# Norm factors by transposes, and the sample tokens' state products issued four units at a time

## The chip, the cores and the metric

The kernel runs on one core of a Trainium2 chip. The metric is the device time of one execution in microseconds (us), the median of several runs. TensorE (PE in the profile; its weight loads are PEld) multiplies matrices into PSUM; VectorE (DVE), ScalarE (ACT) and GpSimd (POOL) do the rest; SP issues nearly all DMAs.

## The reference, cut to what matters

One layer of a hybrid decoder for 1024 prompt tokens and 8 x 8 sample tokens: a SwiGLU feed-forward net, a token mixer with a pooling branch and an SSD (Mamba-2) branch, a second feed-forward net, and a last norm. All is float32.

```python
def rmsnorm(x, g):
    xf = x.astype(jnp.float32)
    y = xf * lax.rsqrt(jnp.mean(xf * xf, axis=-1, keepdims=True) + EPS)
    return (y * g.astype(jnp.float32)).astype(x.dtype)
...
def step(h, inp):
    s_c, d_c = inp
    return h * d_c[..., None, None] + s_c, h
h_last, h_prev = lax.scan(step, h0, ...)
y_off = jnp.einsum('bclgn,bcgrpn,bclgr->bclgrp', cr, h_prev, jnp.exp(a_cs))
y = (y_diag + y_off)
...
yg = yg * lax.rsqrt(jnp.mean(yg * yg, axis=-1, keepdims=True) + EPS)
```

For the sample tokens `h0` is the state of each of the 8 sequences (32 heads of 64 x 128 numbers each, 8 MB in all). It is read, enters `y_off` through the products C h0, and is written back as the new state.

## The kernel before

Channels lie on the 128 partitions and tokens along the rows of a tile. The tokens are done in two halves: half 0 is 512 prompt tokens, half 1 the other 512 and the 64 sample tokens. The stages follow one another: `ffn1`, the mixer for half 0 and then half 1, `ffn2`. Dense products split each float32 operand into a high and a low part and use three products (`products`). The weights are split on ACT (`wh`, line 292) and DVE (`wl`, line 293).

**The order of the work.** The dense products are the backbone. Everything else is written as generators ("chains"). A planner clock `pe[0]` counts what was issued to TensorE: `mm` adds the moving size over 2400, times four for plain float32 operands; `tr` adds 0.107. A chain that yields d is due again when that clock has moved on by d. `tick()`, called after each group of dense products (six in half 1), runs chains that are due, and `finish` runs one to its end without waiting. The program order found so is then scheduled by the compiler, which lets later instructions of an engine pass earlier ones that are not ready in its model and fixes one order for each engine. Tiles come from shared pools: `act` gives 42 buffers of 576 columns to nearly everything in the mixer; `psum("ps", ...)` has four banks there and `psum("pd", ...)` four more for the dense products.

**Norm factors.** `rstd` squares the tiles, sums over partitions with products by `ones` (tile `pss`), takes the power on POOL (line 361), and has a column of factors for each 128 tokens in the small tile `rsm`. To multiply a tile, the factors must lie along the row, the same on every partition: `along` (line 363) does it with one TensorE instruction for each 128 tokens, whose stationary operand is the column repeated 128 times and whose moving operand is the identity. Four go into one bank `prb`, which ACT copies to `r` (line 399). In half 1 a fifth one of 64 rows goes into a corner of `pss` (line 402 copies it). `rstd` is called twelve times: once for each half before the mixer and before `ffn2`, and four times for each half in `gating`.

**The sample tokens' state.** `ssd_group` runs a group of 8 heads: four chunks of 128 prompt tokens, and in half 1 a fifth chunk, the sample tokens, whose second part is `ssd_b` with `smp` true. It has eight units: `bh` (which four sequences) times `pr` (which two heads of the group). For a unit:

- `load` issues the DMA of the state (tile `h0`, shown as `h`; line 1242), two units ahead;
- `turn` makes four transposes on TensorE into bank `ph0T` (line 168 is the body of `tr`) and copies it on ACT to `h0T` (line 1250);
- four products of `Cf` (32 columns of C) with `h0T`, one for each sequence, go to the four 32-partition quarters of bank `pyos`, in columns of unit `pr`;
- one product makes `pnew`, what the tokens add to the state; four DVE instructions (line 1273) combine it with `h0`, and a DMA stores the new state (line 1276);
- after the fourth unit (`pr == 3`) ACT copies `pyos` to `yt` (line 1279), four transposes make `pyT`, and DVE multiplies what is wanted of it into `ea` (line 1285).

`turn` of unit i+1 is called just before `pyos` of unit i, and between units stands `yield STEP_S` (2.5). In `mix_half` this chain is started beside the next group's projections (`proj_group`; conv tiles `pc`, whose raw tile `craw` POOL and ACT fill), the output product of the group before (`pso`), and the four `z` tiles (`pz`); `finish(cs)` after `z_tiles` ends it.

Of the kernel before, what the change touches and what calls it, by code (L numbers as in the profile page):

```python
# [14 lines left out]
P = 128  # L15
# [47 lines left out]
def tile_hybrid_pool_ssd_macaron(  # L63
# [19 lines left out]
    def nm(s):  # L83
        uid[0] += 1
        return f"{s}_{uid[0]}"

    def act(shape=(P, 576), dt=F32, name="a"):
        return sp.tile(list(shape), dt, tag="act", bufs=N_ACT, name=nm(name))
# [25 lines left out]
    def psum(tag="ps", name="ps"):  # L114
        npd = stage["npd"]
        return stage["ps"].tile([P, 512], F32, tag=tag, bufs=npd if tag == "pd" else 8 - npd, name=nm(name))
# [46 lines left out]
    def mm(out, lhsT, rhs, start=True, stop=True, free=False):  # L163
        T.matmul(out, lhsT, rhs, start=start, stop=stop, skip_group_check=free)  # L164
        pe[0] += max(out.free_size(), 64) / 2400.0 * (1 if rhs.dtype == F32R else 4)

    def tr(out, in_, idn):
        T.transpose(out, in_, idn)  # L168
        pe[0] += 0.107
# [7 lines left out]
    ident = cp.tile([P, P], F32, tag="ident", name="ident")  # L177
# [184 lines left out]

    def along(out, r, i, n=P):

        mm(out, r[:n, i : i + 1].broadcast_to([n, P]), ident[:n, :n])

    def rstd(tiles, h, count, out, pace=1.0):

# [28 lines left out]
        for c in range(4):  # L397
            along(pr[:, c * P : (c + 1) * P], sm[:, 0], c)
        S.copy(r[:, :512], pr)
        if h == 1:  # L400
            along(pt[:, 64:128], sm[:, 0], 4, NS)
            S.copy(r[:, 512:], pt[:, 64:128])
# [821 lines left out]
    def ssd_b(h, g, c, a, hold, Cf, y4, dts):  # L1224

        dt, acs, dtd, cd, cdp = dts
        abs_, xp, xd, ea, btok, L, tok = a
        smp = c == 4
        hc = c * NH + g * HPG
        hcs = slice(hc, hc + HPG)  # L1230
        ysl = y4[:, :, tok]
        first = h == 0 and c == 0
        if smp:
            units = [(pr, bh) for bh in range(2) for pr in range(4)]

            def src(u):
                gp = g * 4 + u[0]
                return state_ssm[0, u[1] * 4 : u[1] * 4 + 4, 2 * gp : 2 * gp + 2].rearrange("b h p n -> (h p) b n")

            def load(u):  # L1240
                t = act((P, 4, P), name="h0")
                dma(t, src(u))
                return t

            def turn(h0):
                pt = psum("ps", "ph0T")
                for b in range(4):
                    tr(pt[:, b * P : (b + 1) * P], h0[:, b, :], ident)
                hT = act((P, 4, P), name="h0T")
                S.copy(hT.rearrange("p b n -> p (b n)"), pt)  # L1250
                return hT

            h0s = {0: load(units[0]), 1: load(units[1])}
            yield STEP_S
            hTs = {0: turn(h0s[0])}
            for i, (pr, bh) in enumerate(units):
                if i + 2 < len(units):
                    h0s[i + 2] = load(units[i + 2])
                yield STEP_S
                if i + 1 < len(units):  # L1260
                    hTs[i + 1] = turn(h0s[i + 1])
                hT, h0 = hTs.pop(i), h0s.pop(i)
                gp = g * 4 + pr


                if pr == 0:
                    po = psum("ps", "pyos")
                for b in range(4):
                    mm(po[b * 32 : (b + 1) * 32, pr * P : (pr + 1) * P], Cf[:, 512 + bh * 32 : 544 + bh * 32], hT[:, b, :])
                pn = psum("ps", "pnew")  # L1270
                mm(pn, xd[bh][0][:, pr * P : (pr + 1) * P], xd[bh][1].rearrange("p b n -> p (b n)"))
                for b in range(4):
                    V.scalar_tensor_tensor(h0[:, b, :], h0[:, b, :], cdp[0][:, gp, bh * 4 + b : bh * 4 + b + 1],
                                           pn[:, b * P : (b + 1) * P], op0=ALU.mult, op1=ALU.add)
                dst = new_ssm_s[0, bh * 4 : bh * 4 + 4, 2 * gp : 2 * gp + 2].rearrange("b h p n -> (h p) b n")
                dma(dst, h0)
                if pr == 3:
                    yt = act((P, 512), name="yt")
                    S.copy(yt, po)
                    pt = psum("ps", "pyT")  # L1280
                    for k in range(4):
                        tr(pt[:, k * P : (k + 1) * P], yt[:, k * P : (k + 1) * P], ident)
                    own = bass.AP(pt.tensor, pt.offset, [list(pt.ap[0]), [P, 4], [40, 4], [1, NT]])
                    e = ea[:, :, bh * 32 : (bh + 1) * 32].rearrange("p q (b t) -> p q b t", t=NT)
                    V.tensor_tensor(e, own, e, op=ALU.mult)
        elif not first:
            po = psum("ps", "pyo")
            for pr in range(4):
                mm(po[:, pr * L : (pr + 1) * L], hold[:, pr * P : (pr + 1) * P], Cf[:, tok])
        py = psum("ps", "pyd")  # L1290
        for i in range(HPG):
            m_ = abs_[i // abs_[0].shape[1]][:L, i % abs_[0].shape[1], :]
            hh = slice((i % 2) * HD, (i % 2 + 1) * HD)
            mm(py[hh, (i // 2) * L : (i // 2 + 1) * L], xp[:L, i * HD : (i + 1) * HD], m_)
        pyv = py[:, : 4 * L].rearrange("p (q l) -> p q l", l=L)
        if first:
            V.tensor_tensor(ysl, ysl, pyv, op=ALU.add)
        else:
            if not smp:
                V.tensor_tensor(ea, po.rearrange("p (q l) -> p q l", l=L), ea, op=ALU.mult)  # L1300
            V.tensor_tensor(ea, ea, pyv, op=ALU.add)
            V.tensor_tensor(ysl, ysl, ea, op=ALU.add)
# [22 lines left out]
    def ssd_group(h, g, Bf, Cf, xs4, y4, dts):  # L1325
# [6 lines left out]
        for c in range(4 + h):  # L1332
            ga = ssd_a(h, g, c, Bf, Cf, xs4, dts)
            next(ga)
            yield step
            try:
                next(ga)
            except StopIteration as e:
                a = e.value
            yield step  # L1340
            if prev:
                for w in ssd_b(h, g, *prev, Cf, y4, dts):
                    yield w
            prev = (c, a, ssd_st(h, g, c, a, dts))
        yield step
        for w in ssd_b(h, g, *prev, Cf, y4, dts):
            yield w
# [266 lines left out]
```

## Time and profile before

| | us |
|---|---|
| median of three runs | 2942.32 |
| lowest and highest | 2939.81, 2942.77 |
| profiled execution, device time | 2938.48 |
| its span, first to last instruction | 2936.7 |
| mean granted clock of TensorE | 0.997 |

A row of the timeline gives start, length, engine, line of the code, operation, output and inputs, the shape and the number of instructions merged into it; in square brackets the idle time of the engine ahead of it and what ended that. All engine operations of TensorE go through two helpers, `mm` (line 164) and `tr` (line 168), so rows are told apart by the tile they write. Lengths of single matmuls overlap, since their ends are modelled; what a run of them costs is the time from its first start to the start of what follows.

### The profile page before, as it was taken

Reading aid. Unit: us, or ns where it says so; the run is one execution under the profiler, and the core shown is the slowest. Engines: PE = TensorE matmul, PEld = TensorE weight load, DVE = VectorE, ACT = ScalarE, POOL = GpSimd, SP = SyncE. Lnnn points to the kernel's source line nnn. Section 1 sums busy time; section 2 is a strip of 40 time slices with the busy share of each in tenths; the row PEclk is TensorE's granted clock in tenths of the full one; section 3 lists DMA queues with packets and bytes.
Section 4 is the critical chain, followed back from the end, with each engine's and each line's share of the span. In section 5 each row is a group of like instructions: output and inputs, shape, how many; then the busy total and the mean of one; then the engine's idle time right before and its main releaser. Section 6 shows DMA issues by size and latency. Waiting matters only on the chain. (4 is left out here: it accounts for less than half of the span.)

```text
span 2936.7 us, 50272 instructions
## 1 busy us (share of the span) xinstructions
PE 2887.0 (98%) x18676; PEld 2628.6 (90%) x18676; DVE 1702.4 (58%) x3172; ACT 1206.3 (41%) x2456; POOL 531.0 (18%) x642
## 2 busy tenths in 40 slices
PE   7999999999999999999999999999999999999998
PEld 6999999789988888788999988998999999997898
DVE  6655555434273897777633776867665554453432
ACT  5444444423243665443432444443234444443422
POOL 6444444000000000000000010100035444440000
PEclk9999999999999999999999999999999999999999
DMA  4565554854335888678434556556574532236652
GB/s 133 167 224 182 165 173 133 280 188 137 103 98 174 274 257 267 194 226 289 118 97 151 172 179 187 164 162 180 168 249 154 162 103 75 84 98 211 213 165 72
DMA packets 542267, 501.25 MB, mean 171 GB/s; under 512 B 36388, under 2 KB 391780, under 8 KB 542014
## 3 DMA queue, kind: packets, MB, share of 16 engines
q1 hardware_dynamic: 542006, 498.03, 54.3%
q8 instruction: 147, 2.41, 0.3%
q14 instruction: 98, 0.80, 0.1%
q10 hardware_dynamic: 16, 0.00, 0.0%
HBM read 355.94 MB, written 142.20 MB: 170 GB/s over the span
## 5 line engine op out<-in xcount | busy, mean ns | idle before, releaser
L293 DVE TENSOR_TENSOR wl<-wraw,wh 128x512 fp32r<-128x512 f32 (+1 forms) x416 | 284.5, 685 | 423.5 <-ACT wh L292 408.2
L292 ACT ACTIVATE wh<-wraw 128x512 fp32r<-128x512 f32 (+1 forms) x416 | 256.7, 618 | 637.3 <-PE po L164 235.9
L164 PE MATMUL pw<-X,wh 128*128 128x288 f32 (+1 forms) x1416 | 354.0, 329 | 4.8 <-ACT v L574 3.8
L164 PE MATMUL pw<-X,wl 128*128 128x288 f32 (+1 forms) x936 | 268.7, 287 | 0.0
L164 PEld LDWEIGHTS pw<-X,wh 128*128 128x128 f32 x1416 | 237.6, 188 | 26.8 <-ACT v L574 4.6
L164 PE MATMUL pc<-hl,wh 128*128 128x288 f32 (+1 forms) x1152 | 257.0, 330 | 0.0
L164 PE MATMUL pw<-hl,wh 128*128 128x512 f32 x608 | 220.4, 397 | 0.0
L458 DVE TENSOR_TENSOR wl<-s,wh 128x512 fp32r<-128x512 f32 x168 | 129.9, 774 | 146.4 <-ACT wh L457 124.9
L164 PE MATMUL po<-hh,wh 128*128 128x288 f32 (+1 forms) x800 | 210.4, 323 | 3.4 <-ACT hh L353 3.2
L164 PE MATMUL po<-hh,wl 128*128 128x288 f32 (+1 forms) x800 | 210.2, 322 | 0.4 <-DMA wl<-part 0.4
L164 PE MATMUL po<-hr,wh 128*128 128x288 f32 (+1 forms) x800 | 210.4, 322 | 0.0
L164 PE MATMUL pg<-hl,wh 128*128 128x288 f32 (+1 forms) x864 | 201.6, 338 | 0.8 <-issue 0.8
L164 PEld LDWEIGHTS pc<-hl,wh 128*128 128x128 f32 x1152 | 184.0, 188 | 18.9 <-issue 4.2
L164 PE MATMUL pw<-hi,wh 128*128 128x288 f32 x640 | 189.1, 295 | 1.2 <-ACT t L610 1.2
L164 PE MATMUL pw<-hi,wl 128*128 128x288 f32 x640 | 188.4, 294 | 0.0
L164 PE MATMUL pw<-lo,wh 128*128 128x288 f32 x640 | 188.4, 294 | 0.0
L164 PEld LDWEIGHTS pw<-X,wl 128*128 128x128 f32 x936 | 176.5, 189 | 0.0
L164 PE MATMUL pz<-hl,wh 128*128 128x288 f32 (+1 forms) x768 | 172.2, 333 | 0.0
L164 PE MATMUL pw<-hl,wl 128*128 128x256 f32 x608 | 169.7, 279 | 0.0
L164 PE MATMUL pc<-hl,wl 128*128 128x288 f32 (+1 forms) x576 | 157.6, 327 | 0.0
L164 PEld LDWEIGHTS pg<-hl,wh 128*128 128x128 f32 x864 | 141.2, 189 | 15.6 <-issue 2.5
L458 DVE TENSOR_TENSOR wl<-wraw,wh 128x512 fp32r<-128x512 f32 x126 | 100.2, 795 | 88.7 <-ACT wh L457 82.4
(375 smaller groups left out, 6886.3 us busy)
## 6 DMA issues: line engine op xcount, KB each, us to landing
wh<-part SPq DMA_DIRECT2D x204, 256.0 KB
wl<-part SPq DMA_DIRECT2D x204, 256.0 KB
wraw<-in_ffn_w_in_dram SPq DMA_DIRECT2D x188, 256.0 KB
wraw<-in_w_in_dram SPq DMA_DIRECT2D x180, 256.0 KB
wraw<-in_ffn_w_out_dram SPq DMA_DIRECT2D x120, 256.0 KB
part<-wh SPq DMA_DIRECT2D x112, 256.0 KB
part<-wl SPq DMA_DIRECT2D x112, 256.0 KB
ab<-acsd SPq DMA_DIRECT2D x64, 256.0 KB
```

The source lines that it names most:

```text
L164: T.matmul(out, lhsT, rhs, start=start, stop=stop, skip_group_check=free)
L292: S.activation(wh, raw, AF.Copy)
L293: V.tensor_tensor(wl, raw, wh.bitcast(F32), op=ALU.subtract)
L458: V.tensor_tensor(wl, a, wh.bitcast(F32), op=ALU.subtract)
```

## The change

`along` calls `tr` in place of `mm`, with the same operands. In `ssd_b` the turn of a unit is called ahead of the pause before its own `pnew`, the turned states of four units are kept in a dictionary by `pr`, and when `pr == 3` bank `pyos` is taken and all sixteen products of the four units are issued in a row, unit by unit. A `yield 1.0` stands between the copy to `yt` and the transposes of it.

```diff
     def along(out, r, i, n=P):
 
-        mm(out, r[:n, i : i + 1].broadcast_to([n, P]), ident[:n, :n])
+        tr(out, r[:n, i : i + 1].broadcast_to([n, P]), ident[:n, :n])
...
             h0s = {0: load(units[0]), 1: load(units[1])}
+            hTs = {}
             yield STEP_S
-            hTs = {0: turn(h0s[0])}
             for i, (pr, bh) in enumerate(units):
                 if i + 2 < len(units):
                     h0s[i + 2] = load(units[i + 2])
+                hTs[pr], h0 = turn(h0s[i]), h0s.pop(i)
                 yield STEP_S
-                if i + 1 < len(units):
-                    hTs[i + 1] = turn(h0s[i + 1])
-                hT, h0 = hTs.pop(i), h0s.pop(i)
                 gp = g * 4 + pr
-                if pr == 0:
-                    po = psum("ps", "pyos")
-                for b in range(4):
-                    mm(po[b * 32 : (b + 1) * 32, pr * P : (pr + 1) * P], Cf[:, 512 + bh * 32 : 544 + bh * 32], hT[:, b, :])
                 pn = psum("ps", "pnew")
                 mm(pn, xd[bh][0][:, pr * P : (pr + 1) * P], xd[bh][1].rearrange("p b n -> p (b n)"))
...
                 dma(dst, h0)
                 if pr == 3:
+                    po = psum("ps", "pyos")
+                    for q in range(4):
+                        for b in range(4):
+                            mm(po[b * 32 : (b + 1) * 32, q * P : (q + 1) * P], Cf[:, 512 + bh * 32 : 544 + bh * 32], hTs[q][:, b, :])
+                    hTs = {}
                     yt = act((P, 512), name="yt")
                     S.copy(yt, po)
+                    yield 1.0
                     pt = psum("ps", "pyT")
```

## The prediction

> **What bounds the kernel now.** I read the page's busy shares first, then the busy time by stretch, then what TensorE (PE) waited for.
>
> ```profile
> span 2936.7 us, 50272 instructions
> PE 2887.0 (98%) x18676; PEld 2628.6 (90%) x18676; DVE 1702.4 (58%) x3172; ACT 1206.3 (41%) x2456; POOL 531.0 (18%) x642
> ...
> PE 37%; DMA 1%; DVE 1%; ACT 0%; issue 0%; POOL 0%; SPq 0%; POOLq 0%; ACTq 0%; DVEq 0%
> ```
>
> ```profile
> 1372.00:1650.00 278.00, 277.75 (x2009) 270.15 (x2009) 140.99 (x307) 97.83 (x224) 9.94 (x44) 1.00 0.49 144
> 1650.00:1720.00 70.00, 69.79 (x590) 62.43 (x589) 54.12 (x137) 30.71 (x70) 2.13 (x8) 1.00 0.58 174
> 1720.00:1960.00 240.00, 237.95 (x1911) 221.51 (x1910) 172.90 (x410) 104.88 (x237) 22.55 (x51) 1.00 0.59 176
> 1960.00:2060.00 100.00, 99.49 (x811) 91.92 (x810) 72.60 (x176) 37.50 (x81) 1.55 (x1) 1.00 0.55 162
> ```
>
> ```profile
> PE ptx L164 <- DVE dg L755: 11.6, 2, 11.5
> ...
> PE prb L164 <- POOL rsm L361: 0.7, 1, 0.7
> PE ph0T L168 <- DMA h<-in_state_ssm_dram: 0.6, 2, 0.5
> ```
>
> In the stretch rows the columns are the length, then the busy time of PE, PEld, DVE, ACT and POOL, the granted clock and the DMA share. The stretch from 1650 to 2060 us holds all that the second half of the change touches; PE is busy 407.2 of 410 us there, the next engine (DVE) 299.6. The clock is 1.00, so no gain is to come from there. The longest wait of PE is at the start of the kernel. The part of the chain of waits that the profile follows is PE almost alone. So the rule for the sum is: a microsecond taken off PE's own row of instructions is a microsecond off the end, unless it turns into a new wait.
>
> **Part A: `along` by transposes.** Twelve calls of `rstd` make four factors of 128 rows each, and six of them (the second half) one of 64. Each is a plain f32 product now, which the trace shows as two records.
>
> ```profile
> L164 PE MATMUL prb<-ident,rsm x96: 271/275/377, 690.8 to 2188.2; 128*128 128x128 f32 x96
> L164 PE MATMUL pss<-ident,rsm x12: 272/296/319, 1375.6 to 2188.6; 64*128 64x64 f32 x12
> ```
>
> ```profile
> 690.77 1.05 PE L164 MATMUL prb<-ident,rsm 128*128 128x128 f32 x8
> 691.59 0.51 PE L164 MATMUL po<-hh,wh 128*128 128x288 f32 x2
> ...
> 2027.18 0.60 PE L168 MATMUL ph0T<-ident,h 128*128 128x128 f32 x4
> 2027.53 0.51 PE L164 MATMUL pso<-yh,wh 128*128 128x288 f32 x2
> ```
>
> The ends of matmuls are modelled and overlap, so I take start to next start: the eight records of one call hold PE for 691.59 - 690.77 = 0.82 us. Four transposes of the same shape, in the state turns (`ph0T`), are four records and hold it for 2027.53 - 2027.18 = 0.35 us; both are followed by the same kind of product. Gain 0.47 us a call, 12 x 0.47 = 5.6 us. The 64-row ones lose one record of two; by the record above (0.82 / 8 = 0.10 us) that is 6 x 0.10 = 0.6 us. Part A: 6.2 us. That the weights are one column repeated changes nothing I can see: the product reads the same repeated column now. If a transpose of it didn't pipeline, its bound is the 0.27 us that one record lasts (a rival below).
>
> The Trainium skill (TensorE: Matmul & The Clock Gate, Part 4: PE-mode transpose) gives about 275 ns for one such transpose inside a kernel and speaks against this edit: by that figure, an estimate, four would take 1.10 us and part A would cost 12 x 0.28 = 3.4 us instead. The trace agrees with the length of one record and disagrees with the sum, since the next one starts 0.1 us behind.
>
> **Part B: the products `pyos` of four units together.** There are four groups of heads, each with eight units (a unit: load a state, turn it, `pyos`, `pnew`, update, store). One unit now, and one stretch in which a unit's `pyos` happens to lie elsewhere:
>
> ```profile
> L164 PE MATMUL pyos<-h0T,Cf x256: 272/285/298, 1701.9 to 2050.2; 128*32 128x128 f32 x128
> ```
>
> ```profile
> 1704.65 0.63 PE L168 MATMUL ph0T<-ident,h 128*128 128x128 f32 x4 [0.19 <-DMA h<-in_state_ssm_dram]
> 1705.03 0.48 PE L164 MATMUL pnew<-bblk,X 96*128 96x512 f32 x1
> 1705.35 0.29 PE L164 MATMUL pc<-hl,wl 128*128 128x288 f32 x1
> ...
> 2019.47 1.09 PE L164 MATMUL pyd<-ab,xdt 128*64 128x128 f32 x16
> 2020.49 0.40 PE L164 MATMUL pso<-yh,wh 128*128 128x288 f32 x1
> ...
> 2043.72 0.60 PE L168 MATMUL ph0T<-ident,h 128*128 128x128 f32 x4
> 2044.25 0.43 PE L164 MATMUL pyos<-h0T,Cf 128*32 128x128 f32 x8
> 2044.61 0.50 PE L164 MATMUL pnew<-bblk,X 96*128 96x512 f32 x1
> 2044.94 0.70 PE L164 MATMUL pz<-hl,wh 128*128 128x288 f32 x4
> ```
>
> With `pyos` a unit holds PE for 2044.94 - 2043.72 = 1.22 us; the turn and `pnew` alone took 1705.35 - 1704.65 = 0.70 us. So `pyos` costs 0.52 us in its place: 0.36 us of its own and 0.16 us going in and out of the 32-column form (the turn before it holds 0.53 us here, 0.35 us above). 256 / 8 = 32 such places go. What comes: eight places of 16 products, 32 records. No row shows 16 of this form in a row. The lower bound is by `pyd`, whose products sit side by side in two column halves: 16 records in 1.02 us, so 0.128 us for each pass that fills the array; 16 products in four column quarters are 8 passes, 1.02 us, plus the 0.16 us once: 1.2 us. The upper bound is four times today's 0.36 us plus 0.16: 1.6 us. Gain for four units 4 x 0.52 - 1.2 = 0.9 us (0.5 at the other bound), over eight fours 7.0 us (4.0). I take 7.0: within one set, records of the four quarters already run over each other (8 records of 0.27 us in 0.36 us), and between two sets nothing changes form.
>
> The Trainium skill (TensorEngine Tiling (Array Packing), Key Properties) says that a change of tiling mode drains the engine, and that tiles of one mode work in parallel. The 0.16 us at each way in and out agrees with it; by it the sets join and the sum is the 7.0 us.
>
> That `pnew` now stands before the turn of the next unit has no row. Turn, `pnew`, dense product cost no extra in the 0.70 us row (0.35 for the turn, 0.32 for `pnew`), so I take nothing, with 0.09 us (half the 0.16 us, rounded up) x 32 = 2.9 us as the upper bound and nothing below, as there is no gap to remove.
>
> **What is moved.** The turn comes after `pnew`, its four updates, the store and the next load of the unit before it; it issues four transposes and one ACT copy, and SP's order of store and load does not change. The copy of a turned state must be done before `pyos`; now it has a whole unit. The pause of 1.0 between the copy of `yt` and `pyT` I cost at nothing:
>
> ```profile
> 2039.56 0.59 ACT L1279 COPY yt<-pyos 128x512 f32<-128x512 f32 x1
> 2039.80 0.56 PE L164 MATMUL pz<-hl,wh 128*128 128x288 f32 x3
> 2040.20 0.30 PE L164 MATMUL pz<-hl,wl 128*128 128x288 f32 x1
> 2040.33 0.60 PE L168 MATMUL pyT<-ident,yt 128*128 128x128 f32 x4
> ```
>
> `pz` products stand under that copy already and PE does not stop. Without that cover it would cost the copy's 0.59 us eight times, 4.7 us. The pause makes a group's sample part end up to 2 us later. In group 1 the last `pyd` is followed by 9.85 us of `pz`:
>
> ```profile
> 1828.78 9.85 PE pz L164 x74
> ```
>
> So that is hidden. `along` also counts 0.107 instead of 0.213 in the planner, which moves other work by at most one step of six dense products; I take nothing, within 2 us either way.
>
> **What is late next: the state loads.** A unit's load is issued two units ahead.
>
> ```profile
> 2038.63 0.50 SPq L1242 DMA_DIRECT2D h<-in_state_ssm_dram  x1
> ...
> 2041.44 0.50 SPq L1242 DMA_DIRECT2D h<-in_state_ssm_dram  x1
> ...
> 2043.72 0.60 PE L168 MATMUL ph0T<-ident,h 128*128 128x128 f32 x4
> 2047.16 0.63 PE L168 MATMUL ph0T<-ident,h 128*128 128x128 f32 x4 [0.46 <-DMA h<-in_state_ssm_dram]
> ```
>
> The load of 2038.63 is turned 5.1 us later without a wait; that of 2041.44 was waited for, 0.46 us. Units 0.52 us shorter take up to 1.0 us from this lead. The one late load then costs 1.0 us more, which I take.
>
> **The sum:** 6.2 + 7.0 - 1.0 = 12.2 us. The span goes from 2936.7 to about 2924.5 us. The profiled execution was 2938.48 us, 1.8 us more than its span; the median of the three runs, 2942.32, lies 3.8 us above that. From the median: 2942.3 - 12.2 = 2930 us.
>
> **Rivals.**
> 1. *The sets don't join, and `pnew` pays for its new neighbour.* Part B falls to 4.0 us, less 2.9: 6.2 + 1.1 - 1.0 = 6.3 us, 2936; with one of the two only, 2933. For it: nothing shows 16 in a row. Against it: the 0.36 us. Chance 0.10 for the middle, 2934.
> 2. *The loads set the pace.* If each load took the 5.7 us of the late one, two units could not be shorter than 5.7 us, as now (the turns lie 2.8 us apart); PE's order is fixed, so the time saved in a unit becomes a wait for the load. Then only part A is left: 6.2 us less the 1.0, 2937. For it: one load is late already. Against: it is one of 24 behind the first two of each group. Chance 0.11.
> 3. *The transposes of a repeated column don't overlap.* Four at 0.27 us are 1.09 instead of 0.82 us, so part A costs 12 x 0.27 = 3.2 us: 7.0 - 3.2 - 1.0 = 2.8 us, 2939. This is how the skill's figure would work out here; the 0.35 us of four turns is against it. Chance 0.03.
> 4. *Slower: four turned states are held where two were.* They come from the buffers that the conv tiles' `craw` and the loads share.
>
> ```profile
> 1707.76 0.19 POOL L1073 COPY craw<-chist 128x3 f32<-128x3 f32 x1 [45.84 <-PE pyos L164]
> 1818.27 0.19 POOL L1073 COPY craw<-chist 128x3 f32<-128x3 f32 x1 [50.86 <-PE pyos L164]
> ```
>
> POOL's copy into `craw` waits, at both places, for a `pyos` to give its buffer back. A state now stays up to three units, 3 x 2.8 = 8.4 us, longer; behind the POOL copy stand ACT's evacuation of the conv tile and then PE for lack of a PSUM bank. To come out slower by 0.2% (5.9 us) it must cost 12.2 + 5.9 = 18.1 us, 2.3 us for each of the eight fours. At one unit each, 8 x 2.8 = 22.4 us, the time is 2942.3 + 10.2 = 2953 us. For it: the two rows. Against: the copy of 1818.27 is wanted only by the conv products that follow the `pz` of the row at 1828.78, and the `pyos` bank of PSUM is held for one unit instead of four. Chance 0.12.
>
> **How the numbers follow.** Forecast 0.64 at 2930; rivals 0.10, 0.11, 0.03 and 0.12. About 0.2% (5.9 us, so 2936.4) can be told from no change. Forecast and rival 1 are faster: 0.74. Rivals 2 and 3 lie within: 0.14. Rival 4: slower, 0.12. The range starts at 2924 (the sum without the 1.0 us, 2 us of planner's luck, 3 us for how runs differ) and ends at 2940, behind rival 3; outside lie rival 4 and a little of the forecast.
>
> **What would show it.** `prb` with 48 records instead of 96 and about 0.35 us from its first to the next product; `pyos` with 256 records in eight places of about 1.2 us; turn and `pnew` together 0.7 us; waits of `ph0T` for the load near 1.5 us in all; stretch 1650 to 2060 shorter by about 8 us. Wrong would be: waits of PE for `craw` or `z` by several us (rival 4), `ph0T` waits of 5 us or more (rival 2), `pyos` places of 1.6 us (rival 1), or a change of more than 3 us before the first factor at 690 us, where nothing is touched.

## The result, and the profile after

The changed kernel takes 2927.97 us (median of five runs, 2925.14 to 2932.41) against 2942.57 us before on the same chip; the ratio is 0.995, with a 95% interval of 0.9936 to 0.9965. That is 14.6 us less, by the interval 10 to 19 us; 12.2 us and 2930 us were forecast. In a second measurement it took 2927.06 us against 2943.21 us (ratio 0.9943, 0.9931 to 0.9956). The profiled execution was 2926.27 us with a span of 2924.5 us.

First lines of the page and the chain that ended last, changed kernel:

```profile
span 2924.5 us, 50164 instructions
PE 2873.3 (98%) x18622; PEld 2621.2 (90%) x18622; DVE 1706.2 (58%) x3172; ACT 1208.9 (41%) x2456; POOL 533.3 (18%) x642
...
PE 90%; DMA 4%; DVE 3%; ACT 1%; issue 1%; POOL 1%; SPq 0%; POOLq 0%; ACTq 0%; DVEq 0%
```

PE has 18676 - 18622 = 54 matmuls less, one for each factor of part A (48 + 6), and is 13.7 us less busy; its idle time in the whole span went from 49.7 to 51.2 us, so nearly all of it came off the end. A place at which two kernels can be laid over each other is the same product of each. I use two stretches: from the first product `pdt` of half 0 to the first `pbp` of half 1 (called stretch 0; only part A lies in it), and from there to the sums of the last `rstd` (stretch 1: parts A and B). Busy time by stretch, before:

```profile
791.08:1502.86 711.78, 710.13 (x3726) 598.53 (x3726) 504.09 (x971) 330.30 (x626) 18.52 (x60) 1.00 0.65 202
1502.86:2184.16 681.30, 677.52 (x5322) 643.11 (x5321) 435.45 (x966) 257.83 (x558) 51.33 (x116) 1.00 0.57 175
```

and changed:

```profile
790.18:1499.61 709.43, 707.95 (x3704) 595.87 (x3705) 504.27 (x971) 330.79 (x626) 19.79 (x60) 1.00 0.65 203
1499.61:2172.92 673.31, 668.05 (x5298) 640.66 (x5297) 435.08 (x966) 259.32 (x558) 51.94 (x116) 1.00 0.58 177
```

Stretch 0 is 2.35 us shorter, stretch 1 is 7.99 us shorter; the rest of the 12.2 us of span, 1.9 us, lies outside both. Two calls of part A are in it, and a piece of the profile before that has nothing to do with the change:

```profile
2636.23:2639.64 3.41, 3.41 (x12) 2.84 (x11) 3.41 (x5) 1.23 (x3) 1.55 (x2) 0.50 0.65 234
```

For 3.41 us the granted clock was 0.50, which costs up to 1.7 us; the profile of the changed kernel has no such spell between 42 us and its last 10 us. So whole spans hold more than the change: before the first factor, where nothing was changed, the kernels below lie up to 5 us apart (leaving out `buffers41`, whose first factor stands at another place). In stretch 1 no profile has a spell of lower clock, and in stretch 0 `buffers41` alone has two. So small effects are read in the stretches, and each kernel's median stands beside them.

The pieces themselves, from the timeline of the changed kernel:

```profile
690.31 0.60 PE L168 MATMUL prb<-ident,rsm 128*128 128x128 f32 x4
690.67 0.51 PE L164 MATMUL po<-hh,wh 128*128 128x288 f32 x2
...
2027.69 0.39 PE L164 MATMUL pnew<-bblk,X 96*128 96x512 f32 x1
2027.92 0.60 PE L168 MATMUL ph0T<-ident,h 128*128 128x128 f32 x4
2028.28 0.76 PE L164 MATMUL pz<-hl,wh 128*128 128x288 f32 x4
2028.88 0.43 PE L164 MATMUL pz<-hl,wl 128*128 128x288 f32 x2
2029.15 0.69 PE L164 MATMUL pz<-hl,wh 128*128 128x288 f32 x4
2029.67 0.43 PE L164 MATMUL pz<-hl,wl 128*128 128x288 f32 x2
...
2030.74 0.39 PE L164 MATMUL pnew<-bblk,X 96*128 96x512 f32 x1
2031.06 1.08 PE L164 MATMUL pyos<-h0T,Cf 128*32 128x128 f32 x32
2032.07 0.79 PE L164 MATMUL pz<-hl,wh 128*128 128x288 f32 x4
2032.70 0.43 PE L164 MATMUL pz<-hl,wl 128*128 128x288 f32 x2
```

Four factors hold PE for 0.36 us instead of 0.82 us. `pnew` and the turn hold it for 2028.28 - 2027.69 = 0.59 us. The sixteen products take 2032.07 - 2031.06 = 1.01 us, and `pnew` ahead of them 0.32 us instead of the 0.23 us that it takes ahead of a turn. Four `pz` products hold PE for 0.52 us among their like (2029.15), 0.60 us behind a turn (2028.28) and 0.63 us behind the sixteen (2032.07).

PE's waits in stretch 1, before and then changed (total, times, longest):

```profile
PE pso L164 <- ACT craw L874: 1.2, 1, 1.2
...
PE ph0T L168 <- DMA h<-in_state_ssm_dram: 0.6, 2, 0.5
```

```profile
PE ph0T L168 <- DMA h<-in_state_ssm_dram: 2.1, 3, 1.5
```

The waits for state loads grew by 1.5 us. The longest lies in group 0, whose eight turns stand within 14 us of each other, beside the conv tiles (those of group 3 take 23 us):

```profile
1704.72 0.63 PE L168 MATMUL ph0T<-ident,h 128*128 128x128 f32 x4 [1.49 <-DMA h<-in_state_ssm_dram]
```

### The profile page after: what moved, and what is told of

It is laid out like the page before. It is cut to its first block, busy times and chain, and to the rows that moved or that the text cites. A ratio compares the mean times of both kernels' runs of the same rounds, so it can differ in the third digit from the quotient of the medians.

```text
span 2924.5 us, 50164 instructions
## 1 busy us (share of the span) xinstructions
PE 2873.3 (98%) x18622; PEld 2621.2 (90%) x18622; DVE 1706.2 (58%) x3172; ACT 1208.9 (41%) x2456; POOL 533.3 (18%) x642
## 4 chain that ended last, share of the span: by engine, by line
PE 90%; DMA 4%; DVE 3%; ACT 1%; issue 1%; POOL 1%; SPq 0%; POOLq 0%; ACTq 0%; DVEq 0%
PE pw L164 26%; PE po L164 18%; PE pc L164 9%; PE pg L164 8%; PE pz L164 7%; PE pu L164 5%; PE pso L164 5%; PE pbp L164 3%; PE pwo L164 3%; PE pyd L164 1%; PE pst L164 1%; PE pyo L164 1%; DMA bsel<-in_bsel_dram 1%; PE pgm L164 1%; DMA hr<-hd 1%
```

## The experiments

All stretches come from the profile of the kernel named, as above; "ratio" is to the kernel before on the same chip, with its 95% interval.

| kernel | stretch 0 | stretch 1 | median, ratio |
|---|---|---|---|
| before | 711.78 | 681.30 | |
| changed | 709.43 | 673.31 | 2927.97, 0.995 (0.9936 to 0.9965) |
| `after_again` | 709.05 | 671.32 | 2927.06, 0.9943 (0.9931 to 0.9956) |
| `a_alone` | 709.20 | 682.36 | 2939.04, 0.9995 (0.9986 to 1.0004) |
| `a_again` | 709.93 | 682.09 | one run, 2937.86 |
| `a_same_count` | 709.54 | 683.45 | 2938.27, 0.9984 (0.9975 to 0.9993) |
| `a_early_hist` | 709.58 | 679.05 | 2935.01, 0.9974 (0.9964 to 0.9984) |
| `b_alone` | 711.61 | 673.93 | 2933.77, 0.9975 (0.9966 to 0.9984) |
| `order_alone` | 709.78 | 677.25 | 2932.21, 0.9975 (0.9964 to 0.9986) |
| `pairs` | 709.36 | 674.32 | 2930.23, 0.9964 (0.9951 to 0.9978) |
| `no_pause` | 710.49 | 671.02 | 2929.47, 0.9951 (0.9936 to 0.9966) |
| `buffers41` | 714.21 | 673.42 | 2932.54, 0.9964 (0.9951 to 0.9977) |
| `loads3` | 710.05 | 671.39 | 2927.93, 0.9947 (0.993 to 0.9964) |
| `early_loads` | 709.74 | 670.26 | 2926.32, 0.9943 (0.9929 to 0.9956) |

**Each part by itself.** `a_alone` is the kernel before with `tr` in `along`; `b_alone` is the changed kernel with `mm` there.

> Part A alone (along by transposes, pyos as before). Theory 1, TensorE's own time counts one for one: prb and the 64-row factors together hold PE for 6.9 us instead of 13.6 us, so the span falls by 6 to 7 us, to about 2930, and the median by as much. Theory 2, the gain of the change comes from a better order of the work and not from the shorter instructions: prb falls as said but the span stays within 2 us of 2936.7.

> Part B alone (products of four units together, along by plain products). Theory 1: pyos in eight places of about 1.0 us, turns, pyos and pnew together 7 to 8 us less than before, of which 1.5 to 2 us go back into waits for the state loads; span about 5 to 6 us less than 2936.7. Theory 2 (order of the work): no relation between these terms and the span; the two parts alone don't add up to the 12.2 us of both.

Stretch 1, `b_alone`, then `a_alone`:

```profile
1504.29:2178.22 673.93, 669.87 (x5322) 643.85 (x5321) 434.92 (x966) 258.20 (x558) 51.43 (x116) 1.00 0.57 177
```

```profile
1498.79:2181.15 682.36, 675.08 (x5299) 639.73 (x5297) 435.12 (x966) 258.16 (x558) 52.73 (x116) 1.00 0.57 175
```

Part B behaves in the stretches as theory 1 has it: stretch 1 is 7.4 us shorter, stretch 0 as before. Part A does so in half 0 only (2.6 us for five calls and one corner). In stretch 1 its five calls with four corners are worth 5 x 0.46 us and more, and yet the stretch is 1.1 us longer than before: PE is busy 2.4 us less, and idle for 7.3 us instead of 3.8. The median is 1.4 us lower, within what can't be told from nothing. The spans (2932.6 and 2933.9 us) fit none of the figures expected. By the medians the parts alone don't add up, as theory 2 said (-1.4 and -6.7 against -14.6 us); stretch 1 shows a smaller part of that (+1.1 and -7.4 us against -8.0 and, in the second profile below, -10.0 us). PE's waits in stretch 1, `a_alone`:

```profile
PE pso L164 <- ACT acc L1401: 1.8, 2, 1.1
PE pch L168 <- DMA cin<-in_state_conv_dram: 1.8, 2, 1.6
PE prb L168 <- POOL rsm L361: 1.4, 2, 0.7
```

The longest single wait is that of the conv history's turns (`pch`) for their load. On SP's queue and on PE:

```profile
1617.62 0.40 SPq L1103 DMA_DIRECT2D cin<-in_state_conv_dram  x1
...
1622.98 0.24 PE L168 MATMUL pch<-ident,cin 24*128 24x24 f32 x1 [1.56 <-DMA cin<-in_state_conv_dram]
```

From the issue of the load to the turn it was 5.4 us.

**The same again.** Two yardsticks, unchanged copies of the changed kernel and of `a_alone`.

> The changed kernel once more, as a yardstick: how much the stretch from the first to the last norm factor (10.8 us shorter than before in the first profile) and its waits differ between two profiles of one kernel, and the time beside the two versions below on one chip. If the terms of prb, turn, pyos and pnew are TensorE's own they repeat within 0.3 us; the waits for small loads may differ by 1 to 2 us.

> Part A alone once more, one profile. If the wait of the conv history's turns for their load (1.85 us in group 1 of the first profile, 2.47 us with the other count) is a matter of the order that part A gives, it is there again, over 1 us; if it was an accident of that execution, it is under 0.5 us as before the change.

The changed kernel's stretch 1 differs by 2.0 us between its two profiles, part A's by 0.3 us. In the changed kernel PE's busy time there repeats within 0.2 us (668.05 and 667.89 us), so the 2.0 us are waits; in part A it differs by 1.0 us (675.08 and 676.11 us). PE's waits in stretch 1 of `a_again`:

```profile
PE pso L164 <- ACT acc L1401: 2.3, 2, 1.6
PE ph0T L168 <- DMA h<-in_state_ssm_dram: 1.4, 3, 0.9
...
PE pch L168 <- DMA cin<-in_state_conv_dram: 0.5, 1, 0.5
```

So the 1.56 us of `pch` was largely an accident of that execution, and the stretch is just as long without it: the turns of states waited longer in its place (1.4 us instead of 0.2), so that the two kinds of small loads together were waited for 2.0 us in one profile and 1.9 us in the other, against 0.6 us before. What repeats besides is the wait of `pso` for ACT's copies into `acc` (1.8 and 2.3 us). Neither the kernel before nor the changed one has it, but before the change one of these products waits 1.2 us for ACT too (`craw`), so this accounts for 0.6 and 1.1 us of the loss.

**Was it the planner's count?**

```diff
         tr(out, r[:n, i : i + 1].broadcast_to([n, P]), ident[:n, :n])
+        pe[0] += max(out.free_size(), 64) / 2400.0 * 4 - 0.107
```

> Part A alone, but the planner clock counts each of the transposes as the plain product (0.213 for 128 rows) that it replaces. Part A alone gained 3.0 us in half 0 and lost 1.0 us in half 1, where its own terms are 3.0 us less. If the shorter count moved chains and cost the 4 us, they come back: the stretch from the first to the last factor is 5 to 6 us shorter than before, not 2.0. If the compiler's own schedule did it (it times a transpose differently whatever the planner counts), the stretch stays about 2 us shorter.

By the stretches, no: with the old count stretch 1 is 2.2 us longer than before (from the first to the last factor, the stretch of which the expectation speaks, it is 0.5 us shorter, where 5 to 6 or 2 us were expected). Here `pch` waits 2.2 us, `ph0T` 1.8 us and `prb` 1.4 us. The medians don't settle it: 0.9984 is near the 0.9979 that part A's 6.2 us would make, but its interval overlaps that of `a_alone` (0.9995).

**Was it the conv history's load?** In `a_early_hist` the load of the next group's history (`load_cin`, the three DMAs of tiles `cin`) is issued one dense tile earlier.

```diff
+                if h == 1 and j == 3 and g + 2 < NG:
+                    cins[g + 2] = load_cin(g + 2)
                 pz = dense(W, 0, KD, OFF_Z + (g * 4 + j) * P, xs, name="pz", keep=True)[0]
...
+            if h == 1 and g == 0 and i == 5:
+                cins[1] = load_cin(1)
```

> Part A alone, with the conv history (tiles cin) of a group loaded one dense tile (about 6 us) ahead of where it is turned. If the late load is what ate part A's gain in half 1, the wait of pch falls under 0.3 us and the stretch from the first to the last factor is 4 us shorter than before instead of 2.0. If the loss lies elsewhere in the order, the stretch stays near 2 us.

`pch` no longer waits, nor does `pso` for ACT, and stretch 1 is 2.25 us shorter than before: part A's due there is nearly all paid. The ratio goes from 0.9995 to 0.9974. The expected 4 us from the first to the last factor came out as 4.9 us (1491.8 us against 1496.7). But two things changed at once, the load and, with it, the order, so the load is not shown to be the cause.

**What pays in part B?** In `order_alone` the order of turn and `pnew` is the changed kernel's, but each unit issues its own products; in `pairs` two units do it together.

```diff
-                if pr == 3:
+                if pr == 0:
                     po = psum("ps", "pyos")
-                    for q in range(4):
-                        for b in range(4):
-                            mm(po[b * 32 : (b + 1) * 32, q * P : (q + 1) * P], ..., hTs[q][:, b, :])
+                for b in range(4):
+                    mm(po[b * 32 : (b + 1) * 32, pr * P : (pr + 1) * P], ..., hTs[pr][:, b, :])
```

> As the changed kernel, with its order of turn and pnew and its pause, but each unit's four pyos products issued at once behind its own pnew: 32 places of 8 records again. Theory 1, part B pays because TensorE changes to the 32-column form 8 times instead of 32: that gain falls back, pyos with its ways in and out costs about 0.5 us in each of 32 places again, and the span is 5 to 7 us over the 2924.5 of the changed kernel. Theory 2, part B pays because the turn no longer stands ahead of pyos and its copy has time: the span stays within 2 us of 2924.5.

> As the changed kernel, but the products of two units together: 16 places of 16 records. Theory 1: cost goes with the number of places; each place more costs one way in and out, 0.16 us and the 0.07 us that a set alone takes longer than 2 passes, so 8 more places cost about 2 us: span about 2926.5. A rival in which the sets pay only when all four stand together: span near that of order_alone.

One place of `order_alone`, then one of `pairs`:

```profile
1805.20 0.39 PE L164 MATMUL pnew<-bblk,X 96*128 96x512 f32 x1
1805.53 0.42 PE L164 MATMUL pyos<-h0T,Cf 128*32 128x128 f32 x8
1805.88 0.66 PE L168 MATMUL ph0T<-ident,h 128*128 128x128 f32 x4
1806.29 0.76 PE L164 MATMUL pz<-hl,wh 128*128 128x288 f32 x4
```

```profile
1808.17 0.39 PE L164 MATMUL pnew<-bblk,X 96*128 96x512 f32 x1
1808.50 0.64 PE L164 MATMUL pyos<-h0T,Cf 128*32 128x128 f32 x16
1809.07 0.66 PE L168 MATMUL ph0T<-ident,h 128*128 128x128 f32 x4
```

With the 0.10 us by which `pnew` is longer ahead of `pyos` (0.33 against 0.23), a place costs 0.35 + 0.10 = 0.45 us for one unit, 0.57 + 0.10 = 0.67 us for two and 1.01 + 0.10 = 1.11 us for four. That is a straight line: 0.22 us a unit and 0.23 us a place. What the way out adds to the instruction behind comes on top: 0.05 us to a turn (0.41 us here against 0.36 us), 0.11 us to a `pz` (0.63 against 0.52 us). The sets join, in pairs as well as in fours, so the rival of `pairs` falls; its cost in stretch 1 is 1.0 to 3.0 us over the two profiles of the changed kernel, where 2 were expected. `order_alone` lies between the theories: stretch 1 is 3.9 to 5.9 us longer than with fours, but 5 us shorter than `a_alone`'s. Some of that is the unit's own time (0.33 + 0.35 + 0.41 = 1.09 us against 1.22 us before, of which the next `pz` takes 0.08 us back, so 0.05 us x 32 = 1.6 us), the rest less idle time of PE than part A had alone (3.7 against 7.3 us).

**The pause, the buffers, the loads.** `no_pause` leaves out the `yield 1.0`; `buffers41` sets `N_ACT` to 41; `loads3` issues a state's load three units ahead; `early_loads` is `loads3` with the early conv history.

```diff
-                    yield 1.0
...
-N_ACT, N_PAIR, N_BIG, N_PD = 42, 8, 3, 4
+N_ACT, N_PAIR, N_BIG, N_PD = 41, 8, 3, 4
...
-                if i + 2 < len(units):
-                    h0s[i + 2] = load(units[i + 2])
+                if i + 3 < len(units):
+                    h0s[i + 3] = load(units[i + 3])
```

> The changed kernel without the pause of 1.0 behind the copy of pyos. As the prediction has it, other products stand under the copy with or without the pause: within 2 us of the changed kernel. Rival, the pause is what keeps TensorE from waiting for the copy: up to eight waits of 0.6 us, 2 to 5 us slower.

> The changed kernel with 41 shared buffers instead of 42. If the four held states press on the pool (the slower rival of the prediction), one buffer fewer costs 3 us or more in the second half of the mixer, with waits of POOL and PE around craw. If not, the stretch from the first to the last norm factor is within 2 us of the changed kernel's.

> The changed kernel with each state loaded three units ahead instead of two. Theory 1, the waits of turns for their loads (2.1 us by the waits view, most of it in group 0) are what part B gives back: they fall under 0.5 us and the span falls by 1 to 2 us, to about 2923. Rival, buffers of the shared pool are short once four turned states are held: one more state in flight brings waits elsewhere and the span rises by 2 us or more.

> The changed kernel with both small loads early: states three units ahead and the conv history one dense tile ahead. If waits for loads are what the change gives back, pch and ph0T wait under 1.5 us together and the median is 1 to 3 us under the changed kernel's. Rival: the buffers they hold longer bring other waits, and it is no faster.

The pause does nothing that can be told: stretch 1 without it lies just below the changed kernel's two profiles. One buffer fewer leaves stretch 1 at 673.42 us, where the four states are held, 0.1 and 2.1 us over the changed kernel's two profiles. Stretch 0 is 5 us longer:

```profile
794.38:1508.59 714.21, 712.01 (x3704) 598.98 (x3705) 503.90 (x971) 330.12 (x626) 19.52 (x60) 0.99 0.65 202
1508.59:2182.01 673.42, 667.02 (x5299) 639.53 (x5297) 435.35 (x966) 258.44 (x558) 51.53 (x116) 1.00 0.58 177
```

The number of products is the same, the clock column is not. Two pieces of stretch 0 in the same profile:

```profile
794.38:799.73 5.35, 5.35 (x13) 4.19 (x14) 0.45 (x1) 0.23 (x1) 0.00 (x0) 0.50 0.64 197
1202.50:1205.92 3.42, 3.42 (x12) 2.84 (x11) 3.42 (x8) 2.36 (x4) 0.00 (x0) 0.50 0.75 227
```

At the granted clock of 0.50 one dense product of 512 columns takes 0.42 us from start to start instead of 0.23 us. About 3.7 of the 5 us come of that, and 0.7 us of a longer wait of PE for the split of a weight (`wl`). Nothing here points to a buffer. The execution is the slowest of five; the median's interval overlaps the changed kernel's, so whether one buffer fewer costs anything stays open.

Earlier loads do little: the wait of `ph0T` is 1.2 us in `loads3` (under 0.5 us was expected) and 1.4 us in `early_loads`, against 2.1 and 0.9 us in the two profiles of the changed kernel, and the ratios (0.9947, 0.9943) are the changed kernel's own. No version tried is clearly better than the change.

## Why the prediction was right

**The bound.** That PE's own row sets the end held: the span fell by 12.2 us to 2924.5 us, as the sum said, with PE 13.7 us less busy. That the two figures agree to the tenth is luck: stretch 1 differs by 2 us between two profiles of the changed kernel, and the profile before has the 3.41 us at half the clock, up to 1.7 us of the difference, which no term of the sum stands for.

**Part A, its price.** 0.47 us a call was forecast, 0.82 - 0.36 = 0.46 us measured. The rival by which transposes don't overlap each other is out; four in 0.36 us also settle it against the sum made from the 275 ns of the Trainium skill (TensorE: Matmul & The Clock Gate, Part 4: PE-mode transpose), a figure given there beside one for bf16, where these are float32.

**Part A, its way to the end.** "A microsecond taken off PE's own row is a microsecond off the end" held in half 0 alone. In half 1, part A alone gained nothing: waits of PE in stretch 1 came in its place, for different releasers in two profiles. Together with part B the gain in stretch 1 is 8.0 and 10.0 us, against the 2.4 and 7.65 us of PE's busy time that the two parts took off alone, so there both terms arrived nearly whole. The prediction had this condition ("unless it turns into a new wait") but looked for the new wait at the state loads of part B only.

**Part B, its price.** 0.9 us for each four was forecast. By the rows it is 4 x 1.22 us before, against 4 x (0.59 + 0.08) + 1.11 + 0.11 us now (0.08 and 0.11 us are by how much the first `pz` behind a turn and behind the sixteen products are longer): 4.88 - 3.90 = 0.98 us, 7.8 us over eight fours instead of 7.0. PE's busy time in stretch 1 of `b_alone` says nearly the same: 677.52 - 669.87 = 7.65 us, of which 7.4 us reached the length of the stretch. The place itself is nearly as taken: 1.01 us for the products and 0.21 us for both ways, where 1.02 and 0.16 us were taken. The gain was larger since turn and `pnew` came to 0.67 us a unit and not 0.70.

The Trainium skill (TensorEngine Tiling (Array Packing), Key Properties) says that a change of tiling mode drains the engine, and not a change of tile alone. The trace agrees: 0.23 us goes with the place, whatever the number of sets in it. That a drain is what takes this time is not shown.

**The loads.** 1.0 us more was taken; it is 1.5 us in one profile and 0.3 us in the other. The place was wrong. In group 3, where the prediction saw the late load, the lead did not shrink:

```profile
2034.94 0.43 SPq L1242 DMA_DIRECT2D h<-in_state_ssm_dram  x1
...
2041.77 0.60 PE L168 MATMUL ph0T<-ident,h 128*128 128x128 f32 x4
```

The last load of the group now stands 6.8 us ahead of its turn instead of 5.7 us; the turns lie mostly 3.0 us apart there instead of 2.8, with other products between them. All waits for states lie in group 0, where the turns follow one another closely. The prediction's row at 1704.65 had shown one there already (0.19 us), while its text counted a single late load. The rival in which the loads set the pace fell with it.

**The slower rival.** Holding four states costs nothing that shows in stretch 1, even with one buffer fewer. POOL's copy into `craw` still waits at two places, now once for `pyos` (46.2 us) and once for ACT's copy of a turned state (59.3 us), and no wait of another engine for this copy is in the profile.

**The pause** at nothing: right, by `no_pause`.

**What stays open** is which rule of the order makes part A alone lose about 4 us in half 1. The planner's count is not it by the stretches, but the medians leave that open. It is not the late conv history alone, since `a_again` is as slow with 0.5 us of it. Waits for small loads of both kinds are the larger part of what repeats: 2.0, 1.9 and 4.0 us in `a_alone`, `a_again` and `a_same_count`, against 0.6 us before and in `a_early_hist`, where the gain is there. But the changed kernel has 2.4 and 1.3 us of them and keeps its gain. There is also only one profile of the kernel before, so how much its own stretch 1 varies is not known.

## What to carry to other kernels

A product with the identity that only moves numbers is worth trying in the transpose form: four of the same shape took 0.36 us here instead of 0.82 us. Small products that use part of the array's columns are best put in one row, since each place has a price of its own (0.23 us here, and up to 0.11 us on the instruction behind) beside that of its products. The neighbour matters too: the turn before a place grew by 0.17 us (0.53 against 0.36 us), while `pnew` takes as long ahead of a place (0.32 us) as ahead of a dense product (0.33 us). A gain of a few tenths of a percent on the bounding engine is only had if no new waits come with it: measure each edit alone and with the others, compare like stretches of two profiles instead of whole spans, and look at the granted clock of a stretch before you explain its length.

## What was not expected of the hardware

The time of a row of column-split f32 products is a straight line in its number (0.45, 0.67 and 1.11 us for 8, 16 and 32 records). Loads of the conv history, 72 KB in three DMAs, were used 5.4 us after their issue, with the turn waiting 1.56 us for them, among the queue's weight loads; in another execution of the same kernel the wait was 0.5 us. The granted clock fell to 0.50 for 3.4 or 6.8 us at a time, and after the first 42 us at places that differ between profiles: at 2636 us before the change, at 793 and 1203 us in `buffers41`, at 509 us in the second profile of the changed kernel and nowhere up to 2916 us in its first. What sets these spells off is not shown.
